# RMSNorm with SiLU on one core: loads and stores on separate DMA queues

## The chip, the cores and the metric

The kernel runs on one core of a Trainium2 chip. The metric is the device time of one execution in microseconds; smaller is better. The time before is the median of four runs.

## What is computed

For each row of 2048 values the kernel divides by the root mean square, multiplies by gamma, and applies SiLU. The rows number 8 x 1024 = 8192, everything is float32, and so 67.1 MB go in and 67.1 MB come out.

```python
def reference(x, gamma, eps):          # x: (8, 1024, 2048), gamma: (2048,), eps = 1e-5
    rms = np.sqrt(np.mean(x ** 2, axis=-1, keepdims=True) + eps)
    out = gamma * x / rms
    return (out * (1 / (1 + np.exp(-out)))).astype(np.float32)
```

## The kernel before

The 8192 rows are cut into 16 blocks of 512 rows. A block is one tile `xt` of 128 partitions x 8192 floats (4.194 MB): partition p holds J = 4 consecutive rows of 2048, so each partition's part is 32 KB of contiguous memory. Six buffers of that size exist (`BUFS`), and tiles take them in turn. The tile `grow`, which holds gamma's row for a moment, is taken from the same six, so it occupies the first buffer until gamma has been spread to all partitions.

Three functions make up the work on a block.

- `load(b)` (L49) issues one DMA of 4.194 MB.
- `stats(b)` forms the sum of squares of each of the four rows: three with a Square on ScalarE (L63), the fourth with a multiply-and-reduce on VectorE (L59). GpSimd then forms the variance (L66) and its power of -0.5 (L69), for all four rows of the partition at once.
- `finish(b)` multiplies each row in place by its factor and by gamma on VectorE (L74, four instructions of 2048 columns), applies Silu in place on ScalarE to pairs of rows (L78, two instructions of 4096 columns), and issues the store of the whole block (L79).

The program is written in the order in which the instructions are to stand on each engine (`manual_schedule`); no planner moves them. An engine executes its own instructions in that order and waits on semaphores where data or a buffer is not ready. A DMA issue is one instruction on the queue of the engine that issues it: while it waits, everything behind it on that engine waits too. Before the change, all DMAs are issued by SyncE: gamma's row (L84), the loads of blocks 0 to 3, and from then on store b and load b + 4 in turn (`LEAD` is 4). Statistics run one block ahead: the loop does `stats(b + 1)` and then `finish(b)`.

Of the kernel before, what the change touches and what calls it, by code (L numbers as in the profile page):

```python
# [1 line left out]

# [4 lines left out]

ACT = mybir.ActivationFunctionType
ALU = mybir.AluOpType


@with_exitstack
def kernel(
    ctx: ExitStack,
    tc: tile.TileContext,
    x: bass.AP,
    gamma: bass.AP,
    eps: bass.AP,
    out: bass.AP,
):  # L20

    nc = tc.nc
    P = nc.NUM_PARTITIONS
    f32 = mybir.dt.float32
    x2 = x.flatten_outer_dims()
    o2 = out.flatten_outer_dims()
    n, d = x2.shape
    J = 4  # L30
    BUFS, LEAD = 6, 4
    nblk = n // (P * J)
    xb = x2.rearrange("(b p j) d -> b p (j d)", p=P, j=J)
    ob = o2.rearrange("(b p j) d -> b p (j d)", p=P, j=J)

    singles = ctx.enter_context(tc.tile_pool(name="singles", bufs=1))
    pool = ctx.enter_context(tc.tile_pool(name="pool", bufs=BUFS))
    small = ctx.enter_context(tc.tile_pool(name="small", bufs=4))
    psum = ctx.enter_context(tc.tile_pool(name="psum", bufs=1, space=bass.MemoryType.PSUM))

    g = singles.tile([P, d], f32)
    half = singles.tile([P, J], f32)
    junk_a = psum.tile([P, d], f32, name="junk_a")
    junk_v = psum.tile([P, d], f32, name="junk_v")
    blocks, rstds = {}, {}

    def load(b):
        xt = pool.tile([P, J * d], f32, name="xt")
        nc.sync.dma_start(out=xt, in_=xb[b])  # L49
        blocks[b] = xt  # L50

    def row(b, j):
        return blocks[b][:, j * d:(j + 1) * d]

    def stats(b):
        ss = small.tile([P, J], f32, name="ss")
        for j in range(J):
            if j == J - 1:
                nc.vector.tensor_tensor_reduce(  # L59
                    out=junk_v, in0=row(b, j), in1=row(b, j), scale=1.0, scalar=0.0,  # L60
                    op0=ALU.mult, op1=ALU.add, accum_out=ss[:, j:j + 1])
            else:
                nc.scalar.activation(out=junk_a, in_=row(b, j), func=ACT.Square,  # L63
                                     accum_out=ss[:, j:j + 1])
        var = small.tile([P, J], f32, name="var")
        nc.gpsimd.tensor_scalar(out=var, in0=ss, scalar1=1.0 / d, scalar2=float(eps),  # L66
                                op0=ALU.mult, op1=ALU.add)
        rstd = small.tile([P, J], f32, name="rstd")
        nc.gpsimd.tensor_tensor(out=rstd, in0=var, in1=half, op=ALU.pow)  # L69
        rstds[b] = rstd  # L70

    def finish(b):
        for j in range(J):
            nc.vector.scalar_tensor_tensor(out=row(b, j), in0=row(b, j), scalar=rstds[b][:, j:j + 1],  # L74
                                           in1=g, op0=ALU.mult, op1=ALU.mult)
            if j % 2:
                pair = blocks[b][:, (j - 1) * d:(j + 1) * d]
                nc.scalar.activation(out=pair, in_=pair, func=ACT.Silu)  # L78
        nc.sync.dma_start(out=ob[b], in_=blocks.pop(b))  # L79
        del rstds[b]  # L80

    with tc.manual_schedule():
        grow = pool.tile([P, J * d], f32, name="xt")
        nc.sync.dma_start(out=grow[0:1, 0:d],  # L84
                          in_=bass.AP(tensor=gamma.tensor, offset=gamma.offset, ap=[[d, 1], gamma.ap[0]]))
        for b in range(LEAD):
            load(b)
        nc.gpsimd.memset(half, -0.5)  # L88
        nc.gpsimd.partition_broadcast(g, grow[0:1, 0:d])  # L89
        stats(0)  # L90
        for b in range(nblk):
            if b + 1 < nblk:
                stats(b + 1)
            finish(b)
            if b + LEAD < nblk:
                load(b + LEAD)


# [1 line left out]
_INS = ['x', 'gamma', 'eps']  # L100
_OUTS = [((8, 1024, 2048), 'float32')]

_NUMBERS = {'eps': 9.999999747378752e-06}


# [26 lines left out]
```

## Time and profile before

| | |
|---|---|
| median of 4 runs | 322.15 us (320.75 to 322.25) |
| the profiled execution | 320.75 us, of which the span is 319.0 us |
| bytes moved | 67.12 MB read, 67.11 MB written |
| DMA engines | 98.3% of 16 engines' span, 421 GB/s over the span |
| ACT (ScalarE) busy | 213.8 us, 67% |
| DVE (VectorE) busy | 181.7 us, 57% |
| POOL (GpSimd) busy | 59.5 us, 19% |
| a load, issue to landing | 42.5 us in the median |
| a store, issue to landing | 33.2 us in the median |

The span is the time between the first and the last event that the profiler recorded on the core; the execution's own time has 1.75 us more around it. In the rows of the page with 40 digits, each digit is the busy share of one fortieth of the span (8 us) in tenths. "SPq" is SyncE's queue, in which the DMA issues stand. An arrow such as "<- ACT xt L78" names what ended a wait.

### The profile page before, as it was taken

Reading aid. Unit: us, or ns where it says so; the run is one execution under the profiler, and the core shown is the slowest. Engines: PE = TensorE matmul, PEld = TensorE weight load, DVE = VectorE, ACT = ScalarE, POOL = GpSimd, SP = SyncE. Lnnn points to the kernel's source line nnn. Section 1 sums busy time; section 2 is a strip of 40 time slices with the busy share of each in tenths; the row PEclk is TensorE's granted clock in tenths of the full one; section 3 lists DMA queues with packets and bytes.
Section 4 is the critical chain, followed back from the end, with each engine's and each line's share of the span. In section 5 each row is a group of like instructions: output and inputs, shape, how many; then the busy total and the mean of one; then the engine's idle time right before and its main releaser. Section 6 shows DMA issues by size and latency. Waiting matters only on the chain.

```text
span 319.0 us, 432 instructions
## 1 busy us (share of the span) xinstructions
DVE 181.7 (57%) x96; ACT 213.8 (67%) x130; POOL 59.5 (19%) x38
## 2 busy tenths in 40 slices
DVE  0209998476390944909458193672918549099500
ACT  1349999998484884748757486674857847487800
POOL 0202232204040130402204031040400304022000
DMA  8999999999999999999999999999999999998994
GB/s 313 411 440 407 452 415 423 386 440 419 436 440 427 445 419 440 427 431 441 423 448 411 444 427 436 444 415 444 427 427 448 415 452 423 431 440 382 456 427 201
DMA packets 4612, 134.24 MB, mean 421 GB/s; under 512 B 513, under 2 KB 513, under 8 KB 513
## 3 DMA queue, kind: packets, MB, share of 16 engines
q1 hardware_dynamic: 4610, 134.23, 98.3%
q14 instruction: 2, 0.02, 0.0%
HBM read 67.12 MB, written 67.11 MB: 421 GB/s over the span
## 4 chain that ended last, share of the span: by engine, by line
DMA 59%; DVE 17%; ACT 13%; issue 5%; DVEq 1%; SPq 1%; ACTq 0%
DMA xt<-in_x_dram 59%; DVE xt L74 16%; ACT xt L78 8%; ACT junk_a L63 4%; DVEq L127 1%; SPq L79 0%; DVE ss L59 0%; DVE junk_v L59 0%; SPq L49 0%; SPq L84 0%; DVEq L59 0%; ACTq L63 0%; DVEq L74 0%
## 5 line engine op out<-in xcount | busy, mean ns | idle before, releaser
L74 DVE SCALAR_TENSOR_TENSOR xt<-xt,rstd,g 128x2048 f32<-128x2048 f32 x64 | 146.1, 2346 | 1.1 <-POOL rstd L69 1.1
L63 ACT ACTIVATE junk_a<-xt 128x2048 f32<-128x2048 f32 x48 | 90.3, 1881 | 65.8 <-DMA xt<-in_x_dram 64.8
L78 ACT ACTIVATE xt<-xt 128x4096 f32<-128x4096 f32 x32 | 115.5, 3615 | 23.0 <-DVE xt L74 23.0
L59 DVE CUSTOM_DVE_ANT_0 junk_v<-xt 128x2048 f32<-128x2048 f32 x16 | 36.8, 2300 | 116.9 <-DMA xt<-in_x_dram 116.9
L66 POOL TENSOR_SCALAR var<-ss 128x4 f32<-128x4 f32 x16 | 14.9, 934 | 219.3 <-ACT junk_a L63 207.8
L69 POOL TENSOR_TENSOR rstd<-var,half 128x4 f32<-128x4 f32 x16 | 42.0, 2624 | 1.3
L63 ACT ACTIVATION_READ_ACCUMULATOR junk_a<-xt 128x1 f32 x48 | 8.9, 186 | 0.0
L89 POOL PARTITION_BROADCAST g<-xt x1 | 2.3, 2302 | 8.5 <-issue 8.5
L59 DVE DVE_READ_ACCUMULATOR2_ANT ss<- 128x1 f32 x16 | 2.3, 142 | 0.0
L63 ACT ACT_TABLE_LOAD x1 | 1.3, 1283 | 0.7 <-PEq L113 0.7
L78 ACT ACT_TABLE_LOAD x1 | 1.3, 1283 | 0.0
L88 POOL MEMSET half<- 128x4 f32 x1 | 0.1, 101 | 0.3 <-POOLq L113 0.3
L113 POOL MEMSET const-float32-0.0<- 128x1 f32 x1 | 0.1, 98 | 0.2 <-issue 0.2
L113 POOL MEMSET const-bfloat16-1.0<- 128x1 bf16 x1 | 0.1, 101 | 0.0
L113 POOL MEMSET const-uint8-127<- 128x1 uint8 x1 | 0.1, 101 | 0.0
L113 POOL MEMSET const-float32-1.0<- 128x1 f32 x1 | 0.1, 98 | 0.0
## 6 DMA issues: line engine op xcount, KB each, us to landing
xt<-in_x_dram SPq DMA_DIRECT2D x16, 4096.0 KB, 42.5
out_dram<-xt SPq DMA_DIRECT2D x16, 4096.0 KB, 33.2
xt<-in_gamma_dram SPq DMA_DIRECT2D x1, 8.0 KB
```

The lines of the kernel that those rows point to most:

```text
L59: nc.vector.tensor_tensor_reduce(out=junk_v, in0=row(b, j), in1=row(b, j), scale=1.0, scalar=0.0, op0=ALU.mult, op1=ALU.add, accum_out=ss[ ...
L63: nc.scalar.activation(out=junk_a, in_=row(b, j), func=ACT.Square, accum_out=ss[:, j:j + 1])
L66: nc.gpsimd.tensor_scalar(out=var, in0=ss, scalar1=1.0 / d, scalar2=float(eps), op0=ALU.mult, op1=ALU.add)
L69: nc.gpsimd.tensor_tensor(out=rstd, in0=var, in1=half, op=ALU.pow)
L74: nc.vector.scalar_tensor_tensor(out=row(b, j), in0=row(b, j), scalar=rstds[b][:, j:j + 1], in1=g, op0=ALU.mult, op1=ALU.mult)
L78: nc.scalar.activation(out=pair, in_=pair, func=ACT.Silu)
L88: nc.gpsimd.memset(half, -0.5)
L89: nc.gpsimd.partition_broadcast(g, grow[0:1, 0:d])
L113: nc = _bacc.Bacc("TRN2", target_bir_lowering=False, num_devices=1)
L127: with _tile.TileContext(nc) as tc:
```

## The change

Three things change. The loads stay on SyncE, and the loop now issues load b + 6 after block b, so that a load waits only for its buffer, that is for the landing of store b. The stores are issued by ScalarE, each directly behind the second Silu of its block and ahead of the next block's Squares. Gamma's row is issued by ScalarE as its first instruction; SyncE starts with the loads of blocks 0 to 4, and the load of block 5, which takes the buffer of gamma's row, is written behind the broadcast.

```diff
-    BUFS, LEAD = 6, 4
+    BUFS, LEAD = 6, 6
...
-        nc.sync.dma_start(out=ob[b], in_=blocks.pop(b))
+        nc.scalar.dma_start(out=ob[b], in_=blocks.pop(b))
         del rstds[b]
 
     with tc.manual_schedule():
         grow = pool.tile([P, J * d], f32, name="xt")
-        nc.sync.dma_start(out=grow[0:1, 0:d],
-                          in_=bass.AP(tensor=gamma.tensor, offset=gamma.offset, ap=[[d, 1], gamma.ap[0]]))
-        for b in range(LEAD):
+        nc.scalar.dma_start(out=grow[0:1, 0:d],
+                            in_=bass.AP(tensor=gamma.tensor, offset=gamma.offset, ap=[[d, 1], gamma.ap[0]]))
+        for b in range(LEAD - 1):
             load(b)
         nc.gpsimd.memset(half, -0.5)
         nc.gpsimd.partition_broadcast(g, grow[0:1, 0:d])
+        load(LEAD - 1)
         stats(0)
```

The waits on semaphores follow from this order. A load of block 6 or later waits for the landing of the store that used its buffer. A store waits for its block's Silu, and in some cases also for an earlier transfer that used the same completion semaphore.

## The prediction

> **What bounds the kernel now.** I read the page first, then the SyncE queue's own waits, then the windows, then the end of the timelines.
>
> ```profile
> span 319.0 us, 432 instructions
> DVE 181.7 (57%) x96; ACT 213.8 (67%) x130; POOL 59.5 (19%) x38
> DMA  8999999999999999999999999999999999998994
> GB/s 313 411 440 407 452 415 423 386 440 419 436 440 427 445 419 440 427 431 441 423 448 411 444 427 436 444 415 444 427 427 448 415 452 423 431 440 382 456 427 201
> q1 hardware_dynamic: 4610, 134.23, 98.3%
> ```
>
> No compute engine is above 67%, while the one DMA queue (q1) occupies all 16 engines for 98.3% of the span. The DMA row has no hole except at the two ends. So the time is bytes over rate, plus the ends.
>
> ```profile
> SPq L79 <- ACT xt L78: 275.6, 16, 25.8
> xt<-in_x_dram SPq DMA_DIRECT2D x16, 4096.0 KB, 42.5
> out_dram<-xt SPq DMA_DIRECT2D x16, 4096.0 KB, 33.2
> ```
>
> SyncE stands 275.6 us at its stores (L79) waiting for the Silu, with the next load queued behind the store. That is what the change removes. But a load takes 42.5 us and a store 33.2 us to land, and a block moved every 19.45 us (loads 6 and 15 land at 104.1 and 279.1 in the chain of waits: 175.0 us for 9 periods) means two transfers of 4.194 MB in that time, 9.7 us each, 431 GB/s. Hence about (42.5 + 33.2) / 19.45 = 3.9 blocks are in the queue on average. SyncE waits, the DMA engines do not.
>
> ```profile
> 0.72 0.34 SPq L84 DMA_DIRECT2D xt<-in_gamma_dram  x1
> 1.12 1.89 SPq L49 DMA_DIRECT2D xt<-in_x_dram  x4
> 39.29 0.34 SPq L79 DMA_DIRECT2D out_dram<-xt  x1
> 39.68 0.43 SPq L49 DMA_DIRECT2D xt<-in_x_dram  x1
> 255.54 48.10 SPq L79 DMA_DIRECT2D out_dram<-xt  x4
> ```
> ```profile
> 279.20 1.88 ACT L63 ACTIVATE junk_a<-xt 128x2048 f32<-128x2048 f32 x1 [4.33 <-DMA xt<-in_x_dram]
> 295.14 3.62 ACT L78 ACTIVATE xt<-xt 128x4096 f32<-128x4096 f32 x1 [0.91 <-DVE xt L74]
> 299.66 3.62 ACT L78 ACTIVATE xt<-xt 128x4096 f32<-128x4096 f32 x1 [0.91 <-DVE xt L74]
> ```
>
> The first store starts at 39.29. The last load lands at 279.1; from there a compute chain of 24.2 us leads to the last store's issue at 303.3 (the view of L79's instructions). That store lands 13.8 us later. The first load, with nothing ahead of it, needed 12.3 us, so the last store queued only 1.5 us: that is all the slack the end has.
>
> **The change part by part.**
>
> *Loads ahead of stores on SyncE; lead 6 instead of 4.* Removed: the 275.6 us wait ahead of the loads. Added: load b+6 waits for store b to land, because both use the same of six buffers. A buffer's cycle is 6 x 19.45 = 116.7 us. It is in compute from landing to store issue for 34.8 us (block 14: 259.8 to 294.6) and in the queue for 42.5 + 33.2 = 75.7 us, which leaves 6.2 us between a store's landing and the next load's issue. That is what the change recovers: 6.2/19.45, a third of a block more in a queue of 3.9 blocks. The queue never ran dry in the middle, so I cost it at 0; the cover is those 3.9 blocks. SyncE has only loads left, and a load that waits holds up only later loads, which wait for later stores.
>
> Here a rule speaks against the change. The row is the 275.6 us. The Trainium skill, "DMA: Bandwidth & Descriptors", section "Issuing engines are not separate DMA queues", says that DMAs started by different engines run on the same 16 engines, so a second issuer saves only issue time. By the row's plain reading, up to 275.6 us would be recovered; by the rule, 0. The 98.3% decides for the rule.
>
> *Stores on ScalarE.* Sixteen issues of 0.34 us are added to ACT: 5.4 us on 213.8. Behind each stand the next block's Squares. In the steady part these wait 4.33 us for their load anyway, so 0.34 is hidden. At the start (39 to 59 us) ACT is continuous and stores 1 and 2 come 0.4 to 0.8 us later, behind a queue that holds loads until about 50 us: 0. At the end store 14's issue stands ahead of the last Silu pair, which has 0.91 us of idle before each half, waiting on DVE: 0. The semaphore waits added to some stores refer to transfers some four blocks (78 us) back, landed long before: 0. If covers failed, each issue is worth 0.34 us.
>
> *Gamma on ScalarE.* SyncE's first load issues at 0.72 instead of 1.12: -0.40 us, on the path, since bytes after that are continuous. ACT's table load moves by 0.34, hidden by the 11.48 us before its first Square. Gamma's 8 KB now shares an engine with the loads and can wait behind one 32 KB row: 32,768 B at 431/16 = 26.9 GB/s is 1.2 us. Its consumer is the broadcast at 9.31, and g is first used at 26.5: 0. The sixth load now waits for this broadcast (GpSimd next runs at 23.1 us) while five loads hold the queue to about 50 us: 0 with 27 us in hand.
>
> *Two queues instead of one: the rate.* The trace has one queue, so how two share is unseen. Nearest rows: the mixed stage of before at 431; the 8-us windows of 8 to 64 us average (410+438+422+434+422+418+385)/7 = 418; the best, 72 to 96, average 437. Both rings would be busy from 39 to 277 us, 238 us. At 418 this costs 238 x (431/418 - 1) = +7.4 us; at 437 it gains 3.3. I take 431, 0 us: same engines, same rows, and loads and stores alternate already.
>
> *The end.* Before, the queue order fixes that exactly four stores follow load 15. In the changed kernel the sharing decides. The skill's same page, "Queues, rings and completion order", says each engine goes round-robin between rings packet by packet; no run here shows it yet. Packets are 32 KB rows for both directions, so shares are equal. The windows (last column GB/s) show what is loaded by the time the first store comes, near 40 us:
>
> ```profile
> 0.00:8.00 8.00, 0.00 (x0) 1.28 (x1) 0.29 (x5) 1.00 0.82 312
> 8.00:16.00 8.00, 2.36 (x2) 2.48 (x3) 2.30 (x1) 1.00 0.95 410
> 16.00:24.00 8.00, 0.00 (x0) 3.53 (x4) 0.81 (x2) 1.00 1.05 438
> 24.00:32.00 8.00, 7.73 (x5) 7.69 (x8) 1.98 (x3) 1.00 0.98 422
> 32.00:40.00 8.00, 8.00 (x5) 7.57 (x3) 2.23 (x1) 1.00 1.01 434
> ```
>
> By 40 us that is 8 us x (312+410+438+422+434) GB/s = 16.1 MB = 3.85 loads. From there equal counts: 12.15 loads and 12.15 stores, leaving 3.85 stores after load 15. That is 0.15 x 9.7 = 1.5 us less than four. The 1.5 us slack is gone: I cost the gap at +0.5 (0 to 1.5). With the rule of one ring in issue order instead, it would be 0.
>
> Sum on the profiled execution, 320.75 us (span 319.0 and 1.75 around it): -0.40 + 0.5 = 320.85. The median is 322.15, 1.40 above that execution, so 322.25; I say 322.3.
>
> **The rivals.**
>
> *Stores take more than half (slower).* Place: the end. If a store packet is served a little more readily than a load, the last load lands with fewer stores behind it and the 24.2 us chain lies open. With shares 0.49/0.51, stores move 12.15 x 51/49 = 12.65 while the loads finish: 0.5 block less cover, +4.9 us, 327. At 0.48/0.52 it is 1.0 block, +9.7, 332. It stops there about: stores 14 and 15 cannot be issued before 15.5 and 24.2 us after load 15 lands. It decides from any share of the loads below a half, since the slack is nil. For: the slack. Against: equal rows and fixed turns. Shares above a half for loads cost nothing.
>
> *Alternating rows lower the rate (slower).* 425 GB/s gives 238 x 1.4% = +3.4 us, 325.5. For: the start, with a single kind of traffic at a time, is already as low as 385 to 422 at places. Against: the mixed stage has the steadiest rate.
>
> *Two rings fill each other's bubbles (faster).* At 437, -3.3 us, and no gap: 318.5. For: windows of 440 and more exist. Against: the 98.3% leaves at most 1.7%, 5.4 us, and part of that is the two ends.
>
> *It does nothing but move issues.* This is my forecast.
>
> **How the numbers follow.** Runs of this kernel spread about 0.5%, so less than 0.5% (1.6 us: 320.5 to 323.8) cannot be told from no change. Forecast, 0.38: within it at 322.3 (320.5 to 323.8). Stores ahead at the end, 0.28: 324 to 332. Lower rate, 0.14: 324 to 329. Higher rate, 0.20: 317.5 to 320.5. Faster 0.20, same 0.38, slower 0.42. The range 318.5 to 328.5 leaves out some 0.06 below and 0.11 above.
>
> **What would show it.** Right: a second queue near half of the bytes; first load issued at 0.7; loads 6 to 15 landing about 19.4 us apart; the DMA row at 9 until the last two or three slices; last load landing near 277 to 279 and last store landing under 14 us after its issue. The slower rival: a DMA slice well under 9 between the last load's landing and the last store, load 15 landing after 281, ACT's last chain unchanged at 24 us. A rate change: the spacing of landings away from 19.45 us with the DMA row still full. The forecast is wrong if the spacing moves by over 0.1 us or if the DMA row has a hole in the last quarter.

## The result

| | before | changed kernel |
|---|---|---|
| ratio, with its 95% interval | 1 | 0.9954 (0.9934 to 0.9974) |
| median of all executions | 321.86 us (56) | 328.64 us (35) |
| lowest to highest | 320.75 to 324.25 us | 319.02 to 339.24 us |
| profiled execution | 320.75 us, span 319.0 | 318.89 us, span 317.1 |

The ratio compares only the executions near the quickest of each kernel; of all 35 executions of the changed kernel, 20 took longer than 325 us, which the kernel before did in none of its 56. So the change has two effects, a gain of about half a per cent at the quick end and a spread of 20 us. The prediction gave one number, 322.3, for both.

The page of a quick execution of the changed kernel, with its queues and its DMA issues (engine, count, KB, median us to landing):

```profile
span 317.1 us, 425 instructions
DMA  8999999999999999999999999999999999999995
GB/s 311 422 442 426 434 380 413 455 417 446 430 430 442 418 446 413 455 413 452 417 442 438 422 446 417 442 422 451 417 446 430 430 438 422 442 422 446 413 451 231
q1 hardware_dynamic: 2304, 67.11, 49.7%
q10 hardware_dynamic: 2306, 67.12, 49.1%
xt<-in_x_dram SPq DMA_DIRECT2D x16, 4096.0 KB, 39.5
out_dram<-xt ACTq DMA_DIRECT2D x16, 4096.0 KB, 42.3
```

There are now two queues with half of the bytes each. The DMA row is as full as before. Over slices 11 to 34 of the GB/s row the mean is 432.5, against 432.9 before: the middle of the kernel runs at the same rate. What SyncE waits for has changed. Its own waits (us in total, times, longest):

```profile
SPq L49 <- DMA out_dram<-xt: 222.7, 10, 51.0
```

and its timeline, now a single run of loads:

```profile
0.72 238.88 SPq L49 DMA_DIRECT2D xt<-in_x_dram  x16
```

The 275.6 us behind the Silu have turned into 222.7 us behind the landing of stores. The end, in ScalarE's timeline (start, duration; then what it waited for):

```profile
278.48 1.88 ACT L63 ACTIVATE junk_a<-xt 128x2048 f32<-128x2048 f32 x1 [4.30 <-DMA xt<-in_x_dram]
298.96 3.62 ACT L78 ACTIVATE xt<-xt 128x4096 f32<-128x4096 f32 x1 [0.91 <-DVE xt L74]
302.61 0.34 ACTq L79 DMA_DIRECT2D out_dram<-xt  x1
```

Block 15's first Square starts at 278.48 instead of 279.20 (0.7 us earlier). The chain to the last store's issue is 24.1 us as before. The landing of the last store stands in no view: the shortest store of L79, 12.6 us here and 13.8 us before, is store 14. But a trace also holds every DMA packet: a block's 128 rows of 32 KB, and behind them sixteen packets of 4 bytes, as many as there are DMA engines. Those are read here as the ends of the sixteen parts of a DMA; the last of them comes 0.3 to 0.4 us before the landing in the views (278.0 and 278.4 for load 15). By them the last store ends at 315.6, 12.9 us after its issue, where before it ended at 317.4, 14.1 us after (1.2 us less). 0.7 + 1.2 is the whole difference of the spans, 1.9 us.

The end is still set by bytes, those of the slowest DMA engine: the one that carried the last row of load 15 (begun at 275.6) then moved 32 rows of stores, its share of four stores, without a gap up to 315.6. Half of the sixteen parts had ended by 314.0.

### The profile page after: what moved, and what is told of

The parts are those of the page before. It is cut to its first block, busy times and chain, and to the rows that moved or that the text cites. A ratio compares the mean times of both kernels' runs of the same rounds, so it can differ in the third digit from the quotient of the medians.

```text
span 317.1 us, 425 instructions
## 1 busy us (share of the span) xinstructions
DVE 181.7 (57%) x96; ACT 213.9 (67%) x130; POOL 59.0 (19%) x38
## 4 chain that ended last, share of the span: by engine, by line
DMA 59%; DVE 23%; another core or an unknown queue 4%; ACT 4%; issue 4%; DVEq 1%; POOL 0%; SPq 0%; ACTq 0%; POOLq 0%
DMA xt<-in_x_dram 32%; DMA out_dram<-xt 27%; DVE xt L74 21%; ACT xt L78 3%; DVE junk_v L59 2%; DVEq L128 1%; ACT junk_a L63 1%; POOL rstd L69 0%; DVE ss L59 0%; SPq L49 0%; DVEq L59 0%; DVEq L74 0%; ACTq L63 0%; POOLq L66 0%
```

## The experiments

"Quick" below means an execution at 319 to 321 us, "long" one above 325. Each series was timed beside the kernel before, whose executions lay between 320.5 and 324.6 us in all of them (medians 322.1 to 322.8).

### How two queues share, by itself

Three kernels with all computation left out:

```diff
+    for b in range(nblk):
+        xt = pool.tile([P, J * d], f32, name="xt")          # 5 buffers
+        nc.sync.dma_start(out=xt, in_=xb[b])                # share_act_sp: nc.scalar
+        nc.scalar.dma_start(out=ob[b], in_=src)             # share_act_sp, share_one_queue: nc.sync
```

share_sp_act: 

> All computation is left out: 16 loads of 4.194 MB on SyncE's queue into five buffers, and 16 stores of the same size on ScalarE's queue from one constant buffer, four to five of each kept outstanding, nothing between them. Theory A (one direction gets more than half, rate unchanged): the total stays at 134.2 MB / 431 GB/s + about 4 us of ends = 315 us in every execution, but one direction finishes first; with shares 0.45/0.55 the favoured one ends at about 284 us and the other alone goes on to 315. Theory B (rows of two rings alternating lower the rate): both directions finish within 5 us of each other, and the total is 320 to 335 us, different from execution to execution. If sharing is equal and the rate is 431: both finish within 10 us of each other (the stores begin some 8 us later, after the fill of their buffer), total 315.

share_act_sp: 

> All computation is left out, and the queues are exchanged: the 16 loads on ScalarE's queue, the 16 stores on SyncE's. Theory A, direction decides: the stores are ahead as before if they were ahead with the queues the other way about. Theory A, ring decides: the order of finishing is reversed. Theory B: the same total of 320 to 335 us as with the queues the other way about, both ending together.

share_one_queue: 

> All computation is left out: the same 16 loads and 16 stores, alternating on SyncE's queue alone. Both theories: about 315 us (134.2 MB at 431 GB/s and the ends), executions within 0.5% of each other, loads and stores landing in turn. If this one too spreads over 10 us and more, the spread does not come from the second queue.

| | us | lowest to highest |
|---|---|---|
| share_sp_act | 316.51 | 316.39 to 316.59 (4) |
| share_act_sp | 316.51 | 316.46 to 316.60 (4) |
| share_one_queue | 321.10 | 318.85 to 321.97 (20) |

The DMA issues of share_sp_act:

```profile
xt<-in_x_dram SPq DMA_DIRECT2D x16, 4096.0 KB, 77.4
out_dram<-src ACTq DMA_DIRECT2D x16, 4096.0 KB, 77.4
```

and of share_one_queue:

```profile
xt<-in_x_dram SPq DMA_DIRECT2D x16, 4096.0 KB, 78.3
out_dram<-src SPq DMA_DIRECT2D x16, 4096.0 KB, 78.3
```

With four of each outstanding, a load and a store both take 77.4 us to land: the shares are equal, and which queue carries which direction makes no difference. That agrees with the rule of turns, packet by packet, that the prediction cites (Trainium skill, "DMA: Bandwidth & Descriptors", "Queues, rings and completion order"), and theory A's unequal shares did not occur here. Against one queue the pair costs 77.4/4 = 19.35 us instead of 19.58, 1.2% less. So two full queues do not cost rate, they gain a little, and their times are steadier. The gain is not a steady one: the last two loads of share_one_queue took 77.4 us as well, and between 80 and 280 us it had 41 rows of over 1.3 us, where share_sp_act had one. Theory B finds no support in bare streams either.

### Which part of the change does it

stores_only, the kernel before with one line changed:

```diff
-        nc.sync.dma_start(out=ob[b], in_=blocks.pop(b))
+        nc.scalar.dma_start(out=ob[b], in_=blocks.pop(b))
```

> The kernel before with one line changed: stores on ScalarE. Gamma's row stays first on SyncE and the lead stays 4 in the text; as SyncE no longer holds stores, the loads should run ahead to six buffers all the same. If the second queue alone makes the change: the same spread as the changed kernel (319 to 339 us), its quickest executions 0.4 us longer than the changed kernel's because gamma's issue is back ahead of the loads. If the lead of 6 is what lets the end come apart: executions of 320 to 323 us like the kernel before.

Measured: 319.55 us median (319.18 to 335.5, 10 executions), ratio 0.9912 (0.9882 to 0.9942). It was repeated beside the changed kernel on one chip:

> The changed kernel, timed beside its relatives on one chip. Expected from its earlier executions: the quickest at 319 to 320, more than half above 322, up to 339.

> The kernel before with the stores alone on ScalarE, gamma's row first on SyncE, timed beside the changed kernel. If gamma's place has a part in the long executions (its broadcast begins at 8.6 us here instead of 10.2 to 11.1, and the first store at 39.2 instead of 40.6): most executions at 319 to 320, as in the first series. If it has none: the same proportion of long ones as the changed kernel.

The changed kernel: 321.52 us (318.77 to 338.6), ratio 0.992 (0.9898 to 0.9943), 9 of 20 long. stores_only: 319.97 us (319.1 to 337.0), ratio 0.9937 (0.9914 to 0.9959), 4 of 22 long. So the stores' line alone brings both the gain and the spread; the lead of 6 adds nothing visible, since in stores_only too SyncE holds all loads and issues them as buffers come free. Gamma's place seems to change how often an execution is long: 6 of 32 in the two series of stores_only, against 9 of 20 here and 20 of 35 before. How it does so was not found.

gamma_only, the other part alone:

```diff
-        nc.sync.dma_start(out=grow[0:1, 0:d], ...
+        nc.scalar.dma_start(out=grow[0:1, 0:d], ...
```

> The kernel before with gamma's row alone moved to ScalarE's queue; loads and stores stay on SyncE in the order of before. Forecast of the prediction's step: -0.4 us on 322.8, that is 322.4, with the spread of the kernel before (320.5 to 324.6). Theory C (gamma on the second queue makes the start late at times): executions up to 339 us here as well.

Measured: 322.91 us (321.04 to 323.77) beside 322.4, ratio 1.0002 (0.9985 to 1.0019). The 0.4 us can be neither seen nor excluded (0.1% is within the interval). Long executions did not appear.

### Long executions of the changed kernel

> The changed kernel once more, for its trace when the time is away from 319 us. Theory A (the end is left bare): the DMA row is full until the last load lands, the landings of loads 6 to 15 stay some 19.4 us apart, the last load lands later than 278.4, by half the excess or more, and after it the DMA row has a hole before the last store. Theory B (rate): landings 20 us and more apart, no hole. Theory C (a late start): the first store is issued later than 38.7, by as much as the time is longer, and the row has its hole before that.

> The changed kernel a further time, for a second trace; expectations as for the first look: theory A, a hole in the DMA row between the last load and the last store; theory B, wider spacing without a hole; theory C, a hole ahead of the first store.

> The changed kernel once more, one look. Theory A: the time is the start of the statistics of block 15 plus 40.4 to 42.1 us (as in the traces of the changed kernel so far: 278.5 with 318.9, 277.2 with 319.3, 283.3 with 324.9), whatever the time is, and the DMA row has a hole of the same size as the excess over 319.5. Theory B: the same sum cannot hold, as a lower rate would stretch the stores behind load 15 as well.

They took 319.27, 324.91 and 328.04 us. Two rows of the page of the third, after_look3:

```profile
DMA  8999999999999999999999999999999999995994
GB/s 322 442 414 418 446 386 442 410 430 426 406 430 422 419 426 426 422 434 419 406 446 418 418 438 410 434 438 402 446 414 422 430 422 430 434 438 221 446 398 213
```

and the lines of its timeline in which block 15 begins on VectorE and is stored:

```profile
286.45 2.30 DVE L59 CUSTOM_DVE_ANT_0 junk_v<-xt 128x2048 f32<-128x2048 f32 x1 [8.19 <-DMA xt<-in_x_dram]
310.53 0.34 ACTq L79 DMA_DIRECT2D out_dram<-xt  x1
```

The same of the second, after_look2:

```profile
GB/s 321 454 381 446 442 377 434 430 426 434 418 442 426 431 438 430 430 434 427 430 434 438 418 442 434 426 438 438 422 434 442 422 438 438 426 434 195 450 406 191
```
```profile
283.32 2.30 DVE L59 CUSTOM_DVE_ANT_0 junk_v<-xt 128x2048 f32<-128x2048 f32 x1 [8.02 <-DMA xt<-in_x_dram]
307.40 0.34 ACTq L79 DMA_DIRECT2D out_dram<-xt  x1
```

In both there is a hole, slice 37: the 5 in the DMA row of after_look3, 221 and 195 GB/s. Load 15 has landed late (283.3 and 286.5 instead of 278.5). Store 14 is issued 15.1 us after the statistics of block 15 begin, and by then stores 12 and 13 have run out on most DMA engines. In after_look2 (the windows' last two columns are the DMA share and GB/s):

```profile
290.00:294.00 4.00, 4.00 (x3) 3.62 (x1) 3.19 (x2) 1.00 0.93 401
294.00:298.00 4.00, 4.00 (x3) 3.29 (x1) 0.00 (x0) 1.00 0.17 74
298.35 0.34 ACTq L79 DMA_DIRECT2D out_dram<-xt  x1
```

The sum that after_look3 was to test holds: 286.45 + 41.6 = 328.04, where the earlier traces gave 40.4 (278.53, 318.89), 42.1 (277.22, 319.27) and 41.6 (283.32, 324.91). The time follows load 15's landing. That looks like theory A's bare end, but it is not the chain that sets the time. When the parts end on the sixteen DMA engines (us; first, eighth, last):

| | after, 318.89 us | after_look2, 324.91 us | after_look3, 328.04 us |
|---|---|---|---|
| load 15 | 274.5, 274.9, 278.0 | 271.2, 272.0, 282.8 | 274.9, 277.0, 286.0 |
| last store | 313.9, 314.0, 315.6 | 318.7, 318.8, 321.6 | 321.8, 321.9, 324.7 |

In after_look2 half of load 15 was there by 272.0, earlier than in the quick execution; one DMA engine ended at 282.8, and a load lands with its last part. From there to the end of the last store are 38.8 and 38.7 us, and 32 rows, one engine's share of four stores, take 32 x 1.213 = 38.8. So the slowest engine worked on without a pause, and the hole is in most of the others. The lateness of this engine is the excess over the quick execution: 4.8 us at load 15 of 6.0 in all, and 8.0 of 9.2; the rest is that the quick one needed 37.5 us from there. A shorter chain would have closed the hole, but not ended these executions sooner.

The loads did not fall behind by unequal turns: from 100 to 270 us 1131 rows of loads and 1114 of stores were begun in after_look2, 1125 and 1122 in the quick trace. What fell behind is a part of the DMA engines. In five quick traces of full-size blocks on two queues (after, after_again, after_look, stores_only and its repetition) the first and the last part of load 15 end 3.2 to 4.6 us apart, in the four long ones (after_look2, which at 324.91 is counted with them, after_look3, tail, chain5_two_queues) 11.1 to 16.7. With one queue it is 4.0 to 5.6 (before, gamma_only, chain5_one_queue).

Slow rows are part of it. The median row of 32 KB takes 1213 ns in every one of these traces, but between 80 and 280 us 276 of 2585 rows of after_look3 took over 1.3 us, 31 of 2635 in after_look2, and 11 of 2642 in the quick trace. In after_look3 they are on most engines, so its rate is lower too: 424.1 GB/s over slices 11 to 34 instead of 432.5, and 1236 and 1240 ns for the mean row of loads and stores instead of 1214. That is theory B's lower rate, in this execution. In after_look2 the rate is 432.1; strung together by their times, most of its slow rows lie on one engine, which lost 6 us by them, no other over 2 (an estimate, as the packets do not name their engine). Slow rows alone do not make an execution long: gamma_only has 60 of 2626. Theory C is refuted: the first store of after_look3 was issued at 39.05, 0.4 us later than in the quick trace.

These traces show something else at the start. The prediction had gamma's delay covered. In after_look2 (ScalarE's DMA issue, GpSimd's broadcast and first variance, VectorE's first product):

```profile
0.72 0.53 ACTq L84 DMA_DIRECT2D xt<-in_gamma_dram  x1
11.14 2.30 POOL L89 PARTITION_BROADCAST g<-xt  x1 [10.32 <-issue]
25.45 1.69 POOL L66 TENSOR_SCALAR var<-ss 128x4 f32<-128x4 f32 x1 [12.00 <-issue]
28.32 2.35 DVE L74 SCALAR_TENSOR_TENSOR xt<-xt,rstd,g 128x2048 f32<-128x2048 f32 x1 [1.17 <-POOL rstd L69]
```

The broadcast's row says 2.30 us, but GpSimd's next instruction follows 12.9 to 14.3 us after its start, without a wait that the profile shows. The broadcast starts at 11.14 instead of 9.31, so the first power comes late, VectorE's first product is 1.8 us later than before (28.32 against 26.48), and the first store is issued at 41.13 instead of 39.29. The DMA engines had loads to do, so no time was lost by it here; the quick after_look issued its first store at 40.6, nearly as late.

### The slack of the end, measured

Two more multiply-and-reduce instructions in the statistics of block 15:

```diff
+        if b == nblk - 1:
+            for j in range(2):
+                nc.vector.tensor_tensor_reduce(out=junk_v, in0=row(b, j), in1=row(b, j), ..., accum_out=extra)
```

> The changed kernel with two more multiply-and-reduce instructions on VectorE in the statistics of block 15 (2 x 2.44 = 4.9 us, results unused), in the chain behind the last load. It measures the slack of the end. By the prediction's sum there is none left: the quickest executions become 4.9 us longer, 319.3 to 324. With 1.5 us of slack as before the change: 322.7.

> The kernel before with the same two instructions (4.9 us) in the statistics of block 15. By the prediction the last store queues 1.5 us behind the one ahead of it, so 4.9 - 1.5 = 3.4 us longer than before: 322.4 to 325.8. With no slack: 327.3; with slack of 5 us or more: unchanged.

On one queue the kernel went from 322.2 to 324.0 us, ratio 1.0053 (1.0035 to 1.0071): of 4.9 us, 1.8 came through, so the slack was 3.1 us (2.6 to 3.8 by the interval) and not 1.5. The trace of before shows where it lies: most DMA engines began store 14 at 295.1, some after up to 1.1 us of idling, while the slowest was busy with store 13 until 298.0. On two queues the quickest execution was 320.47 us, against 318.8 to 319.0 without the addition: 1.5 to 1.7 of 4.9, about 3.3 us of slack in the quickest executions. Of the 17, 12 were long, up to 339.88 us (median 332.51). So the quick executions are not at the edge that the prediction saw. In the profiled one, of 334.25 us, the part of load 15 that came last ended at 290.1, and the parts of the last store ended within 0.2 us of each other: with 4.9 us more in it, the chain did set the end.

### Other ends

tail:

```diff
-            if b + 1 < nblk:
+            if b + 1 < nblk - 1:
                 stats(b + 1)
             finish(b)                # block 15: one store behind each of its two Silu
+            if b + 1 == nblk - 1:
+                stats(b + 1)
```

> The changed kernel with another end: block 14 is finished and stored before the statistics of block 15, and block 15 is stored in two halves, each behind its Silu. Store 14 then no longer waits for load 15. Theory A: quick executions stay at 319 to 320 (the chain behind load 15 gets 3.4 us longer, but the last transfer is half as long, 4.9 us less); the long ones lose up to 10 us, so none above 330. Theories B and C: long executions of up to 339 us as in the changed kernel.

Measured: 321.96 us (319.69 to 335.89, 11), ratio 0.9929 (0.9906 to 0.9951). The quick level is as expected, but 5 of 11 were long and 2 of them above 330, so theory A's bound fell. In the profiled execution of 327.88 us half of load 15 had ended by 274.3, its last part at 285.7, and the slowest engine's part of block 15's stores again 38.8 us later, at 324.5, where half of the parts had ended by 317.9. Freeing store 14 from load 15 and halving the last store do not help an engine that is behind.

end_rows shortened the chain further; end_rows_gamma_sp is the same with gamma's row on SyncE.

```diff
+        if b == nblk - 1:
+            for j in range(J):
+                nc.sync.dma_start(out=row(b, j), in_=xb[b][:, j * d:(j + 1) * d])
...
+            last(b)        # block 15: statistics, Silu and store row by row, after store 14
```

> The changed kernel with another last block only: load 15 is four DMAs of one row each, block 14 is finished and stored before block 15 is touched, and each row of block 15 has its own statistics, Silu and store. The chain behind the last row's landing is then about 2.4 + 3.8 + 2.3 + 1.9 = 10.4 us instead of 24.2, and the last store is a quarter as long. Theory A (bare end): the same executions lose up to 14 us of hole and none lies above 325; the quick ones at 318.5 to 319.5. Theory B (the second queue is slower as a whole in some executions): long ones up to 335 remain.

> The same end, with gamma's row back ahead of the loads on SyncE: candidate for the best version. Theory A: 318.5 to 320 in all executions, against 322.2 before. If gamma's place matters for the start: 0.4 us longer at the quickest than end_rows, with less spread.

end_rows: 323.97 us (318.81 to 334.13, 21), ratio 0.9953 (0.9928 to 0.9977), 9 of 21 long. end_rows_gamma_sp: 320.5 us (319.34 to 331.61, 7), ratio 0.9935 (0.9912 to 0.9957), 1 of 7 long. Again the bound of 325 fell, but this kernel is not the clean test it was meant to be. ScalarE's timeline shows why:

```profile
211.01 3.62 ACT L82 ACTIVATE xt<-xt 128x4096 f32<-128x4096 f32 x1 [0.91 <-DVE xt L78]
238.26 0.34 ACTq L83 DMA_DIRECT2D out_dram<-xt  x1
238.71 1.88 ACT L67 ACTIVATE junk_a<-xt 128x2048 f32<-128x2048 f32 x1 [24.08 <-DMA xt<-in_x_dram]
```

Three more loads shift which completion semaphores the stores use, and this store, with its Silu done at 214.6, waited for the landing of load 13 at 238.2. The squares behind it waited too: a new wait of 23.6 us on the engine that now issues the stores. It is inconclusive on the end. It shows what a store's wait can do on ScalarE.

### Half-size blocks

```diff
-    J = 4
-    BUFS, LEAD = 6, 6
+    J = 2
+    BUFS, LEAD = 12, 12           # j2_one_queue: 12, 8 and all DMAs on SyncE
```

> The changed kernel with blocks of half the size: J = 2 rows per partition, 32 blocks of 2.1 MB, twelve buffers, lead 12; same bytes, same queues, same memory. The compute chain behind the last load is then about 12 us instead of 24.2, and the last store takes 4.9 us instead of 9.7. Theory A (the end is left bare when load 15 lands late; the stores that are still to go then cover about 27 us): the chain now needs 12 + 2.6 of cover, some 12 us less, so nearly all executions lie at 317 to 320 us and none above 324. Theory B (the second queue lowers the rate in some executions): long ones of 325 to 339 us remain in the same proportion.

> The kernel before with the same half-size blocks (J = 2, twelve buffers, lead 8), all DMAs on SyncE. The queue before never left the end bare (store 15 queued 1.5 us), so theory A gives no gain beyond the shorter completion: 321 to 323 us. If half-size blocks help for another reason than the end, this one gains as much as its sister with two queues.

j2_two_queues: 323.87 us (323.61 to 324.01, 15), ratio 1.0042 (1.003 to 1.0055). j2_one_queue: 321.8 us (321.48 to 322.39, 22), ratio 0.9989 (0.9978 to 0.9999). No execution of j2_two_queues was long, and its whole series lies within 0.4 us, but the level is 4 us above the upper end of the forecast. The GB/s row of j2_two_queues:

```profile
GB/s 294 432 420 438 385 430 436 430 432 428 434 432 435 426 429 432 434 428 434 428 432 434 429 432 430 436 430 430 432 434 430 430 432 434 430 430 422 314 304 316
```

and two stores and GpSimd's two operations near its end:

```profile
294.42 0.34 ACTq L79 DMA_DIRECT2D out_dram<-xt  x1
296.89 1.29 POOL L66 TENSOR_SCALAR var<-ss 128x2 f32<-128x2 f32 x1 [3.40 <-ACT junk_a L63]
298.27 2.62 POOL L69 TENSOR_TENSOR rstd<-var,half 128x2 f32<-128x2 f32 x1
301.82 0.34 ACTq L79 DMA_DIRECT2D out_dram<-xt  x1
```

The last three slices stand at 304 to 316 GB/s. Loads are done, and a block is delivered every 7.4 us, the pace of the compute chain, where the bytes of half a block need 4.9. In each 7.4 us GpSimd's two small operations take 3.9, which a block of half the size needs as a whole one does. The end is now set by that.

j2_ahead2 mends that, on the base of stores_only:

```diff
+        stats(1)
         for b in range(nblk):
-            if b + 1 < nblk:
-                stats(b + 1)
+            if b + 2 < nblk:
+                stats(b + 2)
...
-            if j == J - 1:
+            if j == J - 1 and b % 2:      # VectorE squares one row in four, as before
```

> Half-size blocks (J = 2, twelve buffers) with stores alone on ScalarE and gamma's row first on SyncE; statistics two blocks ahead, and VectorE takes one row's squares in every second block, one row in four as in the full-size kernels. The chain behind the last load is about 15 us, the last store 4.9 us. Theory A (bare end): no execution above 322, and the quick level of the second queue, 318.5 to 319.5, in all of them, 0.8 to 1.1% below before. If the end is compute-bound again as with half-size blocks and one block ahead: 323 to 324 in all executions. Theory B: executions up to 335 as with full-size blocks.

Measured: 320.34 us (319.96 to 320.88, 7), ratio 0.9932 (0.9906 to 0.9959) beside 322.43. Its DMA row, GB/s row and DMA issues:

```profile
DMA  7999999999999999999999999999999999999897
GB/s 271 438 413 430 379 430 428 434 432 432 430 432 434 430 431 428 432 431 430 434 430 432 432 432 427 428 432 432 434 430 434 432 430 430 428 430 433 374 428 331
xt<-in_x_dram SPq DMA_DIRECT2D x32, 2048.0 KB, 30.6
out_dram<-xt ACTq DMA_DIRECT2D x32, 2048.0 KB, 19.4
```

All its executions lie within 1 us, and none is long. The quickest full-size executions, at 318.8 to 319.5, are 0.8 to 1.5 us quicker than its median, but its slowest, 320.88, is below the changed kernel's median in both of its series (328.64 and 321.52). The medians of stores_only, 319.55 and 319.97, are lower still, but 6 of its 32 executions were long; at that rate 7 without a long one would come by chance about one time in four. The firmer evidence is j2_two_queues, with none long in 15, against 30 of 58 of the changed kernel, and 12 of 17 of chain5_two_queues on the same chip. So halving the block, with twice the buffers, takes the long executions away. In the traces of the two half-size kernels the parts of the last load end 4.3 and 3.4 us apart, and only 0.1% of the rows of 16 KB take over 7% more than the median of 611 ns, where the full-size traces on two queues have 0.3 to 11% that do so over 1213: the DMA engines stay together there. Whether that is owed to the smaller rows or to the queues, which hold less (a store lands 19.4 us after its issue, of which its own bytes need 4.9), these runs do not separate. A shorter end is hardly the reason, since in tail it did not help.

## Why the prediction was wrong

**The start, -0.40.** The first load did go out at 0.72. But gamma_only gained nothing that can be measured. The cover named for gamma's delay was the wrong one: not g's first use at 26.5, but GpSimd's first variance, which stands behind the broadcast. Its cost, put at 0, was 1.8 us of the first store's start in after_look2, without effect on the time because loads filled the queue. The sixth load waited for the broadcast only until 12.7, not until 23.1.

**Loads as buffers come free, 0.** Right. SyncE's wait shrank from 275.6 to 222.7 us and the rate in the middle stayed (432.9, 432.5). The rule that the prediction cites, that a second issuer saves only issue time (Trainium skill, "DMA: Bandwidth & Descriptors", "Issuing engines are not separate DMA queues"), was borne out on this point. It fell short on another, where the measurement decides: two queues moved a bare stream 1.2% quicker than one.

**ScalarE's issues, 0.** Right: the chain behind load 15 is 24.1 us as before.

**The rate, 431.** Right for quick executions and for after_look2. The term's range, 418 to 437, held what two other long ones showed (424 to 427 in after_look3 and tail), but the text took it for a fixed property of two queues, while it differs from execution to execution.

**The end, +0.5.** This step failed, in both directions. Its slack, 1.5 us before the change, measured 3.1; the 13.8 us from which it was taken is store 14's time, and the last store needed 14.1. The slack after, held to be nil, measured about 3.3 in the quickest executions. And the step counted one stream of 431 GB/s, in which 3.85 loads of lead and equal turns fix when load 15 lands. The turns were equal, but the sixteen DMA engines did not keep step: in the long traces the first and the last part of load 15 ended 11.1 to 16.7 us apart, and the load landed with the last, between 283.2 and 290.5, where the quick traces have 277.0 to 278.6. The slowest engine still had its share of four stores to move, 38.8 us, and that set the time in three of the four.

The slower rival has its signs right: a DMA slice under 9 between the last load and the last store, load 15 after 281, an unchanged chain of 24 us. That is luck, since its mechanism was not at work: stores did not take more than half, and in the traces of the changed kernel it was not the bare chain that set the time. The faster rival's range, 317.5 to 320.5, holds the quick executions, but not by a rate of 437: the middle stayed at 432.5.

**The numbers.** The quick level, 0.9954 of 321.86 or 320.4, is 1.9 us below the 322.3 that was given. The sum charged 0.5 for a gap that is not there; the rest is a gain that no term held. The bare streams' 0.23 us per pair, 3.7 us over 16, would be enough for it, but that this is the source is not shown. The median of all executions, 328.64, lies just above the range. Behind it stands the assumption that the changed kernel would spread by 0.5% as the kernel before does. Nothing in a single trace of before speaks for that; it shows the engines 4.0 us apart on one queue, and says nothing of two.

What stays open: why some rows take over 1.3 us, why with two queues of full-size blocks some DMA engines fall behind in some executions and with one queue in none of those traced, and why gamma's place seems to change how often this happens.

## What to carry to other kernels

A DMA lands with the slowest of its sixteen parts, so bytes over a mean rate give the time only while the DMA engines keep step. On one queue they did here; on two, with blocks of 4 MB, not always. Where a DMA-bound kernel spreads, look first at when the parts of its last load end, and only then at the compute chain behind it. When DMA engines are busy from end to end, count on a second queue for about a percent, and time it over many executions, since one trace of a kernel that spreads by 20 us shows its good day. Half-size blocks took the spread away here, but were quick only once the small operations per block no longer set the pace.

## What was not expected of the hardware

- Two queues with one direction each moved the same 134.2 MB in 316.5 us where one queue took 321.1, and with a spread of 0.2 us instead of 3.1.
- The partition broadcast's row shows 2.30 us, and the load that waited for it was issued at that row's end (12.7 us in the first trace of the changed kernel). But GpSimd's next instruction started 12.9 to 14.3 us after the broadcast's start in ten traces, with no wait in the profile that explains it.
- The same program, on the same queues, had 11 of 2642 rows of 32 KB over 1.3 us in one execution and 276 of 2585 in another; the median row took 1213 ns in both.
- The parts of one load on the sixteen DMA engines ended 3.5 us apart in one execution and 11.6 us in another, with 432 GB/s in the middle of both.
